# Second layer's projections with row-scaled half-precision pairs, prepared beside the scan of the third block

## The chip, the cores and the metric

The kernel runs on one NeuronCore of a Trainium2 chip. The metric is the device time of one execution in microseconds. The core has five engines with queues of their own: TensorE (PE; its weight loads are shown as PEld), VectorE (DVE), ScalarE (ACT), GpSimd (POOL) and SyncE (SP), which here only issues DMAs.

## The reference

Two layers over 2048 tokens of width 1024, one batch. The parts that the change touches are the second layer's projections; `h` is the stream after the first layer.

```python
hn = rms_norm(h, g_pre[0]);  h = x + mamba2_mixer(hn, ...)        # layer 1: projections, scan, output

# shared K/V, once
ckv, k_rope = split(rms_norm(h, g_kv_in) @ kv_w_down, [256])      # (1024 x 288)
ckv = rms_norm(ckv, g_ckv);  kv = ckv @ kv_w_up                   # k_nope, v of 16 heads

# layer 2: latent attention
hn = rms_norm(h, g_pre[1])
cq, gate = split(hn @ mla_w_in, [384])                            # (1024 x 1408)
q = rms_norm(cq, g_q) @ mla_w_uq
o = causal_attention(q, k_nope, k_rope, v) * silu(gate)
out = rms_norm(h + o @ mla_w_out, g_final)
```

`rms_norm(h, g)` scales each row of `h` by the inverse root of its mean square and each column by a gain `g`. The gain of a column of `h` is a factor on a row of the weight matrix, and the kernel puts it there.

## The kernel before

**Precision.** A product of two 32-bit matrices is made of three TensorE products: each operand is split into a high and a low part, and `mm3` (lines 83 to 87) adds high x high, high x low and low x high in PSUM. Where the operands are prepared as F32R, the splitting is done by `split` (lines 111 to 119): ScalarE copies the source to the high part, VectorE subtracts that from the source. `pair16` (lines 121 to 124) does the same into two F16 halves. F16 needs factors that bring each row into range: for the first layer `row_scale` makes from the norms of the rows of its weights a power of two per row (`rw`), puts the reciprocal on the activations' gain (`xg`), and takes the remaining common factor out of the results (`un`, `unh`).

**Stages.** The tokens go in four blocks of 512. The first layer (`mamba`, up to about 1550 us) has 16 items, a block `b` by a group `g` each. The loop body of an item runs the scan of that item (`ssd`) and beside it what comes before and after: the output projection of the item before (`outp`), the convolved and gate projections of the item after (`xbc`, `zgate`), and now and then the preparation of the next block. Each of these is a generator; the loop steps through them one after another and lets the scan go on in proportion (20 steps of the scan over the 32 steps of the others). The first block splits its weights to F32R, the second makes half-precision pairs of them (`wpair` with `b == 1`) and keeps them in DRAM (`w16_d`), the third and the fourth load those.

The second layer's projections (`mla`, about 1550 to 2080 us) run over the same four blocks: `mla_kv_down` (288 columns), `mla_cq` (384 columns), `mla_gate` in two halves of 512 channels, and `mla_up`, which makes keys, values and queries and whose steps are interleaved with the gate's, or in the first block with the last output projection of the first layer. The first half of the gate of the first block is done in the last item of `mamba`. The activations of a block come from `prep` (F32R pairs, eight tiles `xT` per block out of eight buffers). Each weight tile of kv-down, latent and gate comes from `wunit`: a DMA on SP's queue to a raw tile, a ScalarE copy that multiplies by the row's gain, a VectorE subtraction. The raw tiles have three buffers (`wraw`), the pairs six (`wsp`), shared with `mla_up` and `outp`; the gate's later halves use the scan's old tiles instead (`y`, `Xd` and `st0` to `st3`). So the same weights are loaded and split again for each of the four blocks. `latent` copies the results of the two narrow projections out of PSUM and norms them.

Attention follows from about 2080 us, then the output projection (`back`) to the end.

**Order.** The Python order of the calls is the order of priority. A planner orders each engine's queue from it, with its own estimate of durations and of when buffers come free; `high_priority(AHEAD)` puts weight loads and splits ahead of it. In attention TensorE's order is the written one.

**Buffers of the third block.** `hx` (four tiles of 128 x 1024) holds rows of the input in the third item of a block, `wraw` is used there only for a small weight of the next block's time steps.

Of the kernel before, what the change touches and what calls it, by code (L numbers as in the profile page):

```python
# [20 lines left out]
P = 128  # L21
# [26 lines left out]
)  # L48
MAGIC = 12582912.0
# [19 lines left out]
class Net:  # L69
    def __init__(self, tc, a):  # L70
        self.tc, self.nc, self.a = tc, tc.nc, a
        self.n = 0
        self.raws, self.turn = ["y", "Xd"], False
# [52 lines left out]
    def raw(self, late):  # L126
        if not late:
            return self.t(self.wp, "wraw", [P, TB], bufs=WRAW)
        self.raws = self.raws[::-1]
        return self.t(self.sp, self.raws[0], [P, TB], bufs=2)  # L130

    def wunit(self, src, n, scale=None, late=False, norm=None):


        with self.tc.high_priority(AHEAD):
            raw = self.raw(late)
            self.nc.sync.dma_start(raw[:, :n], src)
            if late:
                self.turn = not self.turn
                w = [self.t(self.sp, f"st{2 * self.turn + i}", [P, TB], F32R, bufs=1) for i in range(2)]  # L140
            else:
                u = self.unit = self.t(self.wp, "wsp", [P, 2, TB], F32R, bufs=WSP)
                w = [u[:, i, :] for i in range(2)]
# [39 lines left out]
    def row_scale(self):  # L183
# [17 lines left out]
        v.tensor_tensor(self.xg, self.g0, e.bitcast(F32), ALU.mult)  # L201
        q = self.t(self.sm, "rq", [P, KD], bufs=1)
        v.scalar_tensor_tensor(q, self.xg, -1.0, self.xg, ALU.mult, ALU.max)
# [16 lines left out]
        v.tensor_scalar(self.xg, self.xg, both[:, 0:1], None, ALU.mult)  # L220
        v.tensor_copy(self.un, both[:, 1:2])
        v.tensor_scalar(self.unh, both[:, 1:2], 0.5, None, ALU.mult)
        yield
# [51 lines left out]
    def constants(self, cp):  # L275
# [3 lines left out]

        self.mk = cp.tile([P, 2 * P], BF16, name="mk")  # L280
# [5 lines left out]
    def layer_constants(self, cp):  # L286
# [17 lines left out]
        self.xg = cp.tile([P, KD], F32, name="xg")  # L304
        self.un = cp.tile([P, 1], F32, name="un")
# [23 lines left out]
    def mamba(self, cp):  # L329
# [9 lines left out]
        for n, (b, g) in enumerate(items):  # L339
# [10 lines left out]
            if g == G - 2 and b + 1 < NB:  # L350
# [4 lines left out]
                parts += [self.prep16(b + 1), self.steps(b + 1)]  # L355
# [70 lines left out]
    def prep(self, b, gain=None, tag="tr", each=4):  # L426
# [3 lines left out]
        for k in range(KD):  # L430
            ps = self.transposed(xs, k, tag)
            u = self.t(self.xq, "xT", [P, 2, TB], F32R, bufs=8)
            self.split(u[:, 0, :], u[:, 1, :], ps, None if gain is None else gain[:, k:k + 1])
            self.xT[b].append(u)
            if k % each == each - 1:
                yield

    def prep16(self, b):

        xs = self.xn.pop(b)  # L440
        self.xT[b] = []
        for k in range(KD):
            ps = self.transposed(xs, k)
# [3 lines left out]
            self.pair16(w[:, 0, :], w[:, 1, :], ps, self.xg[:, k:k + 1])  # L447
            self.xT[b].append(w)
            if k % 4 == 3:
                yield  # L450
# [298 lines left out]
    def mla(self, early):  # L749
# [5 lines left out]
        for b in range(NB):  # L755
# [25 lines left out]
            after = iter(()) if last else self.prep(NB + b + 1, None, "mm", 1)  # L781
# [58 lines left out]
    def latent(self, banks, width, total):  # L840
# [3 lines left out]
        for i in range(4):  # L844
            nc.scalar.activation(raw[i][:, :total], banks[i][:, :total], AF.Copy)
# [16 lines left out]
    def mla_kv_down(self, b, tables):  # L862

        nc, a = self.nc, self.a
        banks = self.token_gemm(
            self.xT[NB + b],
            lambda k: self.wunit(a["kv_w_down"][k * P:(k + 1) * P, :], 288, self.gk[:, k:k + 1]), 288, "mm")
# [12 lines left out]
    def mla_cq(self, b):  # L880

        w_in = self.a["mla_w_in"]
        banks = self.token_gemm(
            self.xT[NB + b],
# [465 lines left out]
```

## Time and profile before

| | us |
|---|---|
| median of three runs (3192.35 to 3196.06) | 3196.03 |
| profiled execution | 3198.38 |
| its span, first to last instruction | 3196.6 |
| mean granted TensorE clock | 0.997 |
| TensorE busy | 3099.3 (97%) |
| TensorE weight loads busy | 2244.3 (70%) |
| VectorE busy | 2374.5 (74%) |
| ScalarE busy | 2012.7 (63%) |
| GpSimd busy | 606.6 (19%) |
| mean DMA rate | 151 GB/s |

The profile names a group of instructions by line, engine, operation and tiles (out<-in), with its count, its busy time, the mean duration in ns and the idle time of the engine before it with what ended that. Matmuls overlap in the pipeline: a 128 x 512 one is shown with 380 to 410 ns though the next starts after some 216 to 234 ns, so the distance from start to start is what a product costs. L85 to L87 are the three products of `mm3`, L115 and L116 `split` without a scale, L118 and L119 with one, L123 and L124 `pair16`, L137 the weight load of `wunit`, L845 the copy in `latent`, L648 GpSimd's subtraction in the scan.

### The profile page before, as it was taken

Reading aid. Unit: us, or ns where it says so; the run is one execution under the profiler, and the core shown is the slowest. Engines: PE = TensorE matmul, PEld = TensorE weight load, DVE = VectorE, ACT = ScalarE, POOL = GpSimd, SP = SyncE. Lnnn points to the kernel's source line nnn. Section 1 sums busy time; section 2 is a strip of 40 time slices with the busy share of each in tenths; the row PEclk is TensorE's granted clock in tenths of the full one; section 3 lists DMA queues with packets and bytes.
Section 4 is the critical chain, followed back from the end, with each engine's and each line's share of the span. In section 5 each row is a group of like instructions: output and inputs, shape, how many; then the busy total and the mean of one; then the engine's idle time right before and its main releaser. Section 6 shows DMA issues by size and latency. Waiting matters only on the chain.

```text
span 3196.6 us, 51130 instructions
## 1 busy us (share of the span) xinstructions
PE 3099.3 (97%) x17735; PEld 2244.3 (70%) x17735; DVE 2374.5 (74%) x4786; ACT 2012.7 (63%) x5027; POOL 606.6 (19%) x847
## 2 busy tenths in 40 slices
PE   8999998999999999999999999999999999999998
PEld 6777654556655566655878888877777777777777
DVE  6878887777667666767766675578888888888665
ACT  7878566665455464556646554477877778778522
POOL 1222111211121211212111211322221122222100
PEclk9999999999999999999999999999999999999999
DMA  5443657554443345534386655843434434443394
GB/s 176 127 125 121 212 205 239 191 185 152 142 158 126 115 149 178 172 126 135 125 274 232 214 196 192 267 102 79 98 78 85 80 78 97 78 99 98 109 265 156
DMA packets 220403, 482.51 MB, mean 151 GB/s; under 512 B 28976, under 2 KB 66864, under 8 KB 218704
## 3 DMA queue, kind: packets, MB, share of 16 engines
q1 hardware_dynamic: 178336, 353.78, 34.4%
q0 software_dynamic: 41808, 125.47, 16.0%
q8 instruction: 140, 2.29, 0.3%
q14 instruction: 119, 0.97, 0.1%
HBM read 347.02 MB, written 132.12 MB: 150 GB/s over the span
## 4 chain that ended last, share of the span: by engine, by line
PE 64%; DVE 9%; ACT 6%; DMA 6%; issue 2%; POOL 1%; SPq 0%; ACTq 0%; DVEq 0%; POOLq 0%
PE mm L85 13%; PE mm L86 12%; PE mm L87 12%; PE tr L1090 6%; PE tr L1100 3%; PE tr L1101 3%; PE tr L87 3%; PE tr L86 3%; PE tr L85 3%; DVE cacc L495 2%; DMA big<-cumT 1%; PE tr L699 1%; DMA wraw<-in_ssm_w_in_dram 1%; ACT Pr L1075 1%; DMA os<-ri_d 1%
## 5 line engine op out<-in xcount | busy, mean ns | idle before, releaser
L124 DVE SCALAR_TENSOR_TENSOR PTs<-tr,PTs 128x512 f16<-128x512 f32 (+3 forms) x640 | 374.6, 607 | 92.7 <-ACT PTs L123 87.1
L123 ACT ACTIVATE PTs<-tr 128x512 f16<-128x512 f32 (+3 forms) x640 | 328.2, 540 | 141.8 <-PE tr L1090 140.7
L1063 DVE TENSOR_REDUCE mx<-mm 128x1 f32<-128x512 f32 (+2 forms) x631 | 375.3, 607 | 47.2 <-PE mm L87 44.9
L1075 ACT ACTIVATE Pr<-mm,nm 128x512 f32<-128x512 f32 (+2 forms) x631 | 395.1, 635 | 23.2 <-DVE nm L1067 21.4
L1090 PE MATMUL tr<-pack,Pr 128*128 128x128 f32 x2176 | 317.8, 273 | 1.3 <-ACT Os L1107 1.2
L85 PE MATMUL mm<-xT,wsp 128*128 128x512 f16 (+1 forms) x800 | 309.8, 387 | 0.0
L85 PE MATMUL mm<-K,xT 96*128 96x512 f32 (+2 forms) x639 | 287.0, 449 | 23.2 <-ACT Pr L1075 21.6
L86 PE MATMUL mm<-xT,wsp 128*128 128x512 f16 (+1 forms) x800 | 307.0, 384 | 0.0
L87 PE MATMUL mm<-xT,wsp 128*128 128x512 f16 (+1 forms) x800 | 305.7, 384 | 0.2 <-DVE wsp L116 0.2
L1090 PEld LDWEIGHTS tr<-pack,Pr 128*128 128x128 f32 x2176 | 253.2, 141 | 50.0 <-ACT Os L1107 2.0
L85 PE MATMUL mm<-wsp,xT 128*128 128x512 f16 (+2 forms) x640 | 235.9, 370 | 3.8 <-ACT craw L489 2.8
L495 DVE SCALAR_TENSOR_TENSOR cacc<-craw,pack,cacc 128x512 f32<-128x512 f32 x288 | 218.7, 780 | 27.9 <-ACT cacc L493 25.7
L86 PE MATMUL mm<-wsp,xT 128*128 128x512 f16 (+2 forms) x640 | 235.2, 367 | 1.4 <-DVE wsp L124 1.3
L87 PE MATMUL mm<-wsp,xT 128*128 128x512 f16 (+2 forms) x640 | 234.4, 367 | 0.0
L86 PE MATMUL mm<-K,xT 96*128 96x512 f32 (+2 forms) x639 | 231.6, 363 | 0.0
L87 PE MATMUL mm<-K,xT 96*128 96x512 f32 (+2 forms) x639 | 231.4, 362 | 0.0
L1100 PE MATMUL tr<-PTs,xT 128*128 128x512 f16 (+3 forms) x640 | 222.2, 349 | 0.1
L1101 PE MATMUL tr<-PTs,xT 128*128 128x512 f16 (+3 forms) x640 | 219.7, 347 | 0.0
L85 PE MATMUL mm<-wsp,yT 128*128 128x512 f32 x512 | 209.3, 409 | 6.8 <-DMA wsp<-wo_d 4.1
L692 ACT ACTIVATE Xw<-tr,d_wend 128x64 f32<-128x64 f32 x512 | 111.7, 328 | 161.1 <-DVE y L689 134.6
L86 PE MATMUL mm<-wsp,yT 128*128 128x512 f32 x512 | 204.5, 399 | 0.0
L87 PE MATMUL mm<-wsp,yT 128*128 128x512 f32 x512 | 203.8, 399 | 0.0
(419 smaller groups left out, 7363.6 us busy)
## 6 DMA issues: line engine op xcount, KB each, us to landing
wsp<-wo_d SPq DMA_DIRECT2D x96, 512.0 KB, 3.6
wraw<-in_ssm_w_in_dram SPq DMA_DIRECT2D x128, 256.0 KB, 3.2
big<-cumT SPq DMA_DIRECT2D x64, 512.0 KB, 4.8
wsp<-w_d SPq DMA_DIRECT2D x64, 512.0 KB, 3.8
wo_d<-wsp SPq DMA_DIRECT2D x32, 512.0 KB, 3.6
w_d<-wsp SPq DMA_DIRECT2D x32, 512.0 KB, 3.6
xT<-qn_d POOLq DMA_DIRECT2D x64, 256.0 KB, 4.7
K<-kn_d POOLq DMA_DIRECT2D x15, 1024.0 KB, 8.5
```

The source lines that it names most:

```text
L85: mm(out, l_hi, r_hi, start=start, stop=False)
L86: mm(out, l_hi, r_lo, start=False, stop=False)
L87: mm(out, l_lo, r_hi, start=False, stop=stop)
L123: self.nc.scalar.activation(hi, src, AF.Copy, scale=scale)
L124: self.nc.vector.scalar_tensor_tensor(lo, src, scale, hi, ALU.mult, ALU.subtract)
L495: nc.vector.scalar_tensor_tensor(acc, raw[:, k:k + TB], wk[k], acc, ALU.mult, ALU.add)
L692: act(Xw[:, hc], px[:, hc], AF.Copy, scale=wend[:, h0 + h:h0 + h + 1])
L1063: v.tensor_reduce(mx[:, n:n + 1], s[:, :w], AX.X, ALU.max)
L1075: nc.scalar.activation(x[:, :w], s[:, :w], AF.Exp, bias=nm, accum_out=sm[:, n:n + 1])
L1090: nc.tensor.transpose(pt[:, j * P:(j + 1) * P], st["P"][j][kb], self.ident)
L1100: nc.tensor.matmul(st["O"][:, c], vals[h][:, kb, :], u[:, 0], start=kb == 0, stop=False)
L1101: nc.tensor.matmul(st["O"][:, c], vals[h][:, kb, :], u[:, 1], start=False, stop=kb == nk - 1)
```

## The change

The second layer's projections take F16 pairs. New is `keep2(ks)`: for the row tiles `ks` of the two weight matrices it loads 128 rows (gate columns to one `hx` tile, latent and kv-down columns to another), sums the squares of each row with its gains on ScalarE (three squares), makes from them a power of two per row on VectorE, splits four pieces into F16 pairs with that factor and the gain (`wraw` tiles), and stores them in the new DRAM tensor `w2_d`; each store is issued after the next piece's split. After the last tile `common`, cut out of `row_scale`, makes the activations' factors `xg2` and the common factors `un2` and `unh2`. `beside` steps `keep2` once per step of `zgate` and runs the remaining steps when `zgate` is done. It stands in the items of the third block: row tiles 0 to 2 with its first group, 3 to 5 with the second, 6 and 7 with the fourth. `w2` loads the pairs: two row tiles per DMA to a `wsp` tile, or one per DMA to one of four tiles `st0` to `st3` where the gate came late before. The activations come from `prep16` (four buffers per block), the common factor leaves with the copy in `latent`, the gate's tanh and the output scale `us`.

```diff
-    def wunit(self, src, n, scale=None, late=False, norm=None):
+    def wunit(self, src, n, scale=None, norm=None):
...
-            if late:
-                self.turn = not self.turn
-                w = [self.t(self.sp, f"st{2 * self.turn + i}", [P, TB], F32R, bufs=1) for i in range(2)]
-            else:
...
+    def keep2(self, ks):
+        nc, v, a = self.nc, self.nc.vector, self.a
+        held = []
+        for k in ks:
+            rows = slice(k * P, (k + 1) * P)
+            A, B = (self.t(self.hh, "hx", [P, D], bufs=4) for _ in range(2))
+            nc.sync.dma_start(A, a["mla_w_in"][rows, 384:1408])
+            nc.sync.dma_start(B[:, 0:384], a["mla_w_in"][rows, 0:384])
+            nc.sync.dma_start(B[:, 384:672], a["kv_w_down"][rows, :])
+            yield
+            g1, gk = self.g1[:, k:k + 1], self.gk[:, k:k + 1]
+            n = self.t(self.sm, "kn", [P, 4])
+            junk = self.t(self.wp, "wraw", [P, D], BF16, bufs=WRAW)
+            for i, (x, g) in enumerate(((A, g1), (B[:, 0:384], g1), (B[:, 384:672], gk))):
+                nc.scalar.activation(junk[:, :x.shape[1]], x, AF.Square, scale=g, accum_out=n[:, i:i + 1])
+            v.tensor_reduce(n[:, 3:4], n[:, 0:3], AX.X, ALU.add)
+            v.tensor_scalar(n[:, 3:4], n[:, 3:4], TINY * TINY, None, ALU.max)
...
+            v.tensor_tensor(f[:, 1:2], f[:, 0:1], g1, ALU.mult)
+            v.tensor_tensor(f[:, 2:3], f[:, 0:1], gk, ALU.mult)
+            yield
+            for x, g, at in ((B[:, 384:672], 2, KV2), (B[:, 0:384], 1, CQ2),
+                             (A[:, 0:512], 1, GA2), (A[:, 512:1024], 1, GA2 + 1024)):
+                c = x.shape[1]
+                u = self.t(self.wp, "wraw", [P, 2, c], F16, bufs=WRAW)
+                self.pair16(u[:, 0], u[:, 1], x, f[:, g:g + 1])
+                held.append((self.w2_d[rows, at:at + 2 * c].rearrange("p (s c) -> p s c", s=2), u))
+                if len(held) > 1:
+                    nc.sync.dma_start(*held.pop(0))
+                yield
+        nc.sync.dma_start(*held.pop(0))
+        if ks[-1] == KD - 1:
...
+            self.common(self.xg2, self.un2, self.unh2)
+            yield
+
+    def beside(main, more):
+        for _ in main:
+            next(more, None)
+            yield
+        for _ in more:
+            pass
+
+    def w2(self, at, n, k, late=False):
+        nc = self.nc
+        with self.tc.high_priority(AHEAD):
+            if late:
+                self.turn = (self.turn + 1) % 4
+                u = self.t(self.sp, f"st{self.turn}", [P, 1, 2, n], F16, bufs=1)
+                nc.sync.dma_start(u[:, 0], self.w2_d[k * P:(k + 1) * P, at:at + 2 * n].rearrange(
+                    "p (s c) -> p s c", s=2))
+                return [u[:, 0, i, :] for i in range(2)]
+            if k % 2 == 0:
+                u = self.w16 = self.t(self.wp, "wsp", [P, 2, 2, n], F16, bufs=WSP)
+                nc.sync.dma_start(u, self.w2_d[k * P:(k + 2) * P, at:at + 2 * n].rearrange(
+                    "(j p) (s c) -> p j s c", j=2, s=2))
+        return [self.w16[:, k % 2, i, :] for i in range(2)]
...
-                parts.append(self.prep(NB))
+                parts.append(self.prep16(NB, self.xg2))
...
+            elif b == NB - 2:
+                parts[-1] = self.beside(parts[-1], self.keep2({0: (0, 1, 2), 1: (3, 4, 5), 3: (6, 7)}[g]))
...
-            after = iter(()) if last else self.prep(NB + b + 1, None, "mm", 1)
+            after = iter(()) if last else self.prep16(NB + b + 1, self.xg2, "mm", 1)
...
-            nc.scalar.activation(raw[i][:, :total], banks[i][:, :total], AF.Copy)
+            nc.scalar.activation(raw[i][:, :total], banks[i][:, :total], AF.Copy, scale=self.un2)
...
-            lambda k: self.wunit(a["kv_w_down"][k * P:(k + 1) * P, :], 288, self.gk[:, k:k + 1]), 288, "mm")
+        banks = self.token_gemm(self.xT[NB + b], lambda k: self.w2(KV2, 288, k), 288, "mm")
...
+        banks = self.token_gemm(self.xT[NB + b], lambda k: self.w2(CQ2, 384, k), 384, "tr")
...
-            return self.wunit(self.a["mla_w_in"][k * P:(k + 1) * P, c0:c0 + 512], 512, self.g1[:, k:k + 1], b + n > 0)
+            return self.w2(GA2 + n * 1024, 512, k, b + n > 0)
...
-            nc.scalar.activation(sz, bank, AF.Tanh, scale=0.5)
+            nc.scalar.activation(sz, bank, AF.Tanh, scale=self.unh2)
...
+            v.tensor_scalar(us, us, self.un2, None, ALU.mult)
```

More of the change, by code (lines that the diff above doesn't have):

```diff
@@ L48 @@
 )
+KV2, CQ2, GA2, ALL2 = 0, 576, 1344, 3392
 MAGIC = 12582912.0
@@ L72, in __init__ @@
         self.n = 0
-        self.raws, self.turn = ["y", "Xd"], False
+        self.turn = 0
     def name(self, s):
@@ L354, in mamba @@
                     parts = parts[1:] + parts[:1] + [self.row_scale()]
-                parts += [self.prep16(b + 1), self.steps(b + 1)]
+                parts += [self.prep16(b + 1, self.xg), self.steps(b + 1)]
                 total += 3
@@ L424, in load_x, with prep, prep16 @@
                     nc.vector.tensor_scalar(v, v, r[:, i:i + 1], None, ALU.mult)
-    def prep(self, b, gain=None, tag="tr", each=4):
+    def prep(self, b, gain):
+        xs = self.xn.pop(b)
+        self.xT[b] = []
+        for k in range(KD):
+            ps = self.transposed(xs, k)
+            u = self.t(self.xq, "xT", [P, 2, TB], F32R, bufs=8)
+            self.split(u[:, 0, :], u[:, 1, :], ps, gain[:, k:k + 1])
+            self.xT[b].append(u)
+            if k % 4 == 3:
+                yield
+    def prep16(self, b, factors, tag="tr", each=4):
         xs = self.xn.pop(b)
@@ L431, in prep @@
             ps = self.transposed(xs, k, tag)
[L432 to L443, printed above, removed]
             if k % 2 == 0:
```

52 lines of the change are left out of this document (29 added, 23 removed).

## The prediction

> **What bounds the kernel now.** I read the page's first two parts, then a table of the stretches that the change touches, then the groups of instructions and the order of time inside them.
>
> ```profile
> PE 3099.3 (97%) x17735; PEld 2244.3 (70%) x17735; DVE 2374.5 (74%) x4786; ACT 2012.7 (63%) x5027; POOL 606.6 (19%) x847
> PE   8999998999999999999999999999999999999998
> PEclk9999999999999999999999999999999999999999
> ```
>
> TensorE is busy nearly everywhere at the full granted clock. So the time falls only if TensorE's stream gets shorter or its few gaps close, and it rises only if new gaps open. Columns of the next table: length, then busy us (and count) of PE, PEld, DVE, ACT, POOL, then clock, DMA share, GB/s.
>
> ```profile
> 40.00:360.00 320.00, 314.97 (x1744) 249.94 (x1743) 255.03 (x461) 252.63 (x670) 64.03 (x79) 1.00 0.43 132
> 400.00:790.00 390.00, 368.82 (x2154) 219.50 (x2152) 306.73 (x530) 248.29 (x588) 72.88 (x93) 0.99 0.59 194
> 490.00:590.00 100.00, 90.52 (x502) 52.83 (x501) 73.70 (x125) 60.19 (x138) 18.95 (x24) 0.98 0.64 212
> 815.00:905.00 90.00, 90.00 (x534) 54.23 (x533) 57.91 (x97) 45.98 (x117) 18.43 (x24) 1.00 0.51 176
> 905.00:995.00 90.00, 89.60 (x531) 53.99 (x530) 57.79 (x97) 46.24 (x118) 18.83 (x24) 1.00 0.38 129
> 1105.00:1190.00 85.00, 82.79 (x513) 52.12 (x512) 59.42 (x116) 48.23 (x124) 13.31 (x15) 1.00 0.42 141
> 1550.00:1640.00 90.00, 83.84 (x451) 71.90 (x450) 55.32 (x135) 42.63 (x91) 13.22 (x21) 0.98 0.60 195
> 1640.00:2082.00 442.00, 439.33 (x2175) 371.04 (x2174) 291.56 (x558) 233.21 (x432) 87.04 (x142) 1.00 0.69 226
> ```
>
> Rows 1 and 2 are the first and second blocks of tokens, row 3 the worst stretch of the second. Rows 4 to 6 are the scans of the third block beside which the new work is put: TensorE idles 0, 0.4 and 2.2 us there, 2.6 us of 265. Rows 7 and 8 are the second layer's projections: 6.2 us idle while they start, then 2.7 us of 442. They are a pure TensorE stretch, so a faster matmul there should arrive in the total.
>
> **Part 1: the matmuls' type.** The kv-down, query-latent and gate projections turn from pairs of 32-bit to pairs of half-precision operands; their number stays: three products of 8 row tiles by 4 banks by 4 blocks, 384 each of 288 and of 384 columns, and twice that, 768, of 512 columns. First a stretch of 32-bit products (columns: start, duration), then one of half-precision ones in the first layer.
>
> ```profile
> 1905.05 0.39 PE L85 MATMUL tr<-xT,st 128*128 128x512 f32 x1
> ...
> 1909.71 0.40 PE L87 MATMUL mm<-yT,wsp 128*128 128x512 f32 x1
> ```
>
> ```profile
> 821.82 0.38 PE L85 MATMUL mm<-wsp,xT 128*128 128x512 f16 x1
> ...
> 823.98 0.38 PE L86 MATMUL mm<-wsp,xT 128*128 128x512 f16 x1
> ```
>
> The first pair has 20 starts between its rows: 4.66 / 20 = 233 ns from start to start. The second has 10: 2.16 / 10 = 216 ns. So 17 ns go from each of 768 products: 13.1 us. The groups kept apart by shape (busy us, mean ns) give the rest:
>
> ```profile
> L85 PE MATMUL tr<-xT,st 128*128 128x512 f32 x128 | 52.2, 408 | 0.0
> L86 PE MATMUL tr<-xT,st 128*128 128x512 f32 x128 | 50.4, 394 | 0.0
> L85 PE MATMUL mm<-xT,wsp 128*128 128x512 f16 x576 | 218.9, 380 | 0.0
> L85 PE MATMUL tr<-wsp,xT 128*128 128x384 f32 x128 | 43.1, 337 | 0.0
> L1100 PE MATMUL tr<-PTs,xT 128*128 128x384 f16 x64 | 20.9, 326 | 0.0
> L87 PE MATMUL mm<-wsp,xT 128*128 128x288 f32 x128 | 37.2, 295 | 0.0
> L1100 PE MATMUL tr<-PTs,xT 128*128 128x256 f16 x64 | 17.6, 275 | 0.0
> ```
>
> The ends are modelled, so I use only differences of like groups. 384 columns: 337 against 326, 11 ns by 384 = 4.2 us. 288 columns have no half-precision row: between 275 (256 columns) and 326 (384) lies 275 + 32 x 51 / 128 = 288, against 295; 7 ns by 384 = 2.7 us. The first product of a triple after transposes of 32-bit tiles is longer (408 against 394, so 14 x 128 = 1.8 us) and the half-precision rows show no such thing. Part 1 is 13.1 + 4.2 + 2.7 + 1.8 = **21.8 us gained**; 13.1 if only the wide ones gave, 28.0 if the 768 narrow ones gave 17 ns each too.
>
> The Trainium skill, TensorE: Matmul & The Clock Gate (Wait — 56ns, not 53.3ns?), puts a warm stream at columns / 2.4 + 2.5 ns, 215.7 ns for 512, whatever the operands. By it part 1 would be nothing and the sum below +1.7 us, 3198; the 233 ns above decide against that, so it gets no chance of its own, and the half-precision 216 agree.
>
> **Part 2: the splitting of weights leaves the projections.** One ScalarE copy and one VectorE subtraction for each of 128 weight tiles go (64 for the gate, 32 and 32 for the narrow ones):
>
> ```profile
> L118 ACT ACTIVATE wsp<-wraw,pack 128x384 fp32r<-128x384 f32 x32 | 18.7, 615 | 20.2 <-DMA wraw<-in_mla_w_in_dram 14.2 <-PE mm L87 4.2 <-PE tr L87 1.3
> L118 ACT ACTIVATE wsp<-wraw,pack 128x288 fp32r<-128x288 f32 x32 | 17.0, 536 | 26.6 <-DMA wraw<-in_kv_w_down_dram 18.8 <-PE mm L87 7.2
> ```
>
> With 0.72 for a gate tile (the 512-column copy in part 3), ScalarE loses 64 x 0.72 + 32 x 0.615 + 32 x 0.536 = 83 us, VectorE about as much. They were covered by TensorE, so in themselves worth nothing. They do cost at the start, where three raw buffers serve kv-down, query latent and up-projection in turn. ScalarE, then TensorE:
>
> ```profile
> 1589.15 0.63 ACT L115 ACTIVATE wsp<-wraw 128x512 fp32r<-128x512 f32 x1 [2.40 <-DMA wraw<-in_kv_w_up_dram]
> ```
>
> ```profile
> 1590.22 0.66 PE L271 MATMUL tr<-pack,xs 128*128 128x128 f32 x4 [2.00 <-ACT xs L845]
> ...
> 1592.12 0.63 PE L86 MATMUL mm<-wsp,yT 128*128 128x512 f32 x1
> 1592.55 0.63 PE L87 MATMUL mm<-wsp,yT 128*128 128x512 f32 x1
> ```
>
> ScalarE stands 2.40 us for an up-projection weight; the latent's copies (L845) queue behind, and TensorE loses 2.00 us and then starts products 0.43 us apart instead of 0.23, at the half clock that shows as 0.98 in row 7: 2.0 + 0.02 x 90 = **3.8 us**. With kv-down and query latent off the raw buffers that weight can be fetched long before, so I book all of it. Bounds: 0, and the whole idle of that row with the clock loss, 6.2 + 1.8 = 8.0. What is late next there is the first layer's last output weights, a wait that I leave:
>
> ```profile
> PE mm L85 <- DMA wsp<-wo_d: 4.1, 3, 1.9
> ```
>
> The DMAs: as many bytes (two half-precision halves are as long as one 32-bit word), 92 loads instead of 128 (kv-down and query latent by pairs of tiles). Nothing on TensorE. Likewise the activations' half-precision pairs take four buffers per block instead of eight, and the scale from a column costs ScalarE some 0.1 us a copy, hidden as above.
>
> **Part 3: the new work beside the third block.** `keep2` does three row tiles in each of the first two scans, two in the fourth. Per row tile: two 32-bit loads' worth in three DMAs, three squares with sums (1024, 384, 288 columns), nine column-sized VectorE operations, four pairs (288, 384, 512, 512), four stores. Nearest rows:
>
> ```profile
> L263 ACT ACTIVATE yt<-hx 128x1024 bf16<-128x1024 f32 x28 | 29.2, 1045 | 3.9 <-DMA hx<-in_x_dram 3.8
> L263 ACT ACTIVATE yt<-xs 128x384 bf16<-128x384 f32 x16 | 8.2, 528 | 0.1
> L263 ACT ACTIVATION_READ_ACCUMULATOR yt<-xs 128x1 f32 x32 | 6.5, 205 | 0.0
> L123 ACT ACTIVATE wsp<-wraw,rw 128x512 f16<-128x512 f32 x64 | 45.1, 720 | 26.2 <-DMA wraw<-in_ssm_w_in_dram 24.5 <-PE tr L93 1.5
> L124 DVE SCALAR_TENSOR_TENSOR wsp<-wraw,rw,wsp 128x512 f16<-128x512 f32 x64 | 48.9, 773 | 16.2 <-ACT wsp L123 16.0
> L119 DVE SCALAR_TENSOR_TENSOR wsp<-wraw,pack,wsp 128x384 fp32r<-128x384 f32 x32 | 19.2, 615 | 13.6 <-ACT wsp L118 13.5
> L119 DVE SCALAR_TENSOR_TENSOR wsp<-wraw,pack,wsp 128x288 fp32r<-128x288 f32 x32 | 16.4, 515 | 24.9 <-ACT wsp L118 24.9
> L254 DVE SCALAR_TENSOR_TENSOR rsy<-rsq,rsy 128x4 f32<-128x4 f32 x105 | 16.7, 159 | 2.3
> ```
>
> ScalarE: 1.05 + 0.53 + 0.45 (an estimate for 288 from the 384 row) + 3 x 0.2 + 2 x 0.72 + 0.615 + 0.536 = 5.2 us, by eight 42 us. VectorE: 2 x 0.773 + 0.615 + 0.515 + 9 x 0.16 = 4.1 us, by eight 33 us. Over the three scans ScalarE goes from 140.4 to 182 us of 265 (0.69), VectorE from 175.1 to 208 (0.78). No product waits for any of it, so by itself it is hidden in what those engines have left. But a scan's own chain runs over both, and `beside` hands out one step of `keep2` per step of the gate projection (8), while three tiles have 18 steps: some ten steps come in one heap before the scan's tail and the next scan. What such a load costs is read from two stretches. Row 1 has VectorE at 255 / 320 = 0.80 and ScalarE at 0.79, and TensorE idles 5.0 / 320 = 1.6%. Row 2 has 0.79 and 0.64 and idles 21.2 / 390 = 5.4%, but there its own weights are being split and products wait for them. On 265 us: 4.2 to 14.4 us, less today's 2.6, so +1.6 to +11.8. I take **+5**, a third of the way, since no product waits for `keep2`.
>
> Loads and stores: three tiles are 2.6 MB in and 2.6 MB out per 90 us, 58 GB/s on top of 176 and 129. The projections live with 226 GB/s at 0.6% idle, so no term. The two TensorE instructions of `common` come once; I book +0.5 for them, between 0 and 2.
>
> **Sum**: -21.8 - 3.8 + 5 + 0.5 = -20.1. The profiled execution took 3198.4 us (span 3196.6); 3198.4 - 20.1 = 3178.3. The runs' median, 3196.0, lies 2.4 below that execution, so 3175.9; I say **3176**. With all bounds: -28.0 - 8 + 1.6 = -34.4 to -13.1 + 11.8 + 2 = +0.7, 3162 to 3197; the likeliest case's own range, with not all of them at one end, is 3166 to 3189.
>
> **Rivals.** (A) *The scan's chain gives it back.* Each chunk's state goes through GpSimd's subtractions:
>
> ```profile
> L648 POOL TENSOR_TENSOR Sp<-st,Sp 128x512 fp32r<-128x512 f32 x15 | 22.0, 1468 | 52.4 <-ACT Sp L647 52.3
> ```
>
> ```profile
> L648 POOL TENSOR_TENSOR Sp<-st,Sp 128x512 fp32r<-128x512 f32 x8 | 10.2, 1276 | 24.0 <-ACT Sp L647 24.0
> ```
>
> The first row is the second block (400 to 790), the second the third (815 to 995): beside half-precision splitting the same operation is 0.19 us longer. With ScalarE's and VectorE's queues late as well, the scans could fall to the worst stretch, 9.5 idle of 100: 265 x 0.095 - 2.6 = 22.6 us, so -21.8 - 3.8 + 22.6 + 0.5 = -2.5, 3193.5, no change. Against it: row 1, as loaded, idles 1.6%. The Trainium skill, SBUF — State Buffer (Who interferes with whom), holds that VectorE with two SBUF inputs and GpSimd lock each other out of a shared port pair for a whole instruction. By it, 32 subtractions of up to 0.77 us could hold GpSimd 25 us in all, about the same time; the 0.19 us that rows show is a quarter of one such instruction.
>
> (B) *The projections become bound by something else*, the evictions or stores of the up-projection, and half of part 1 turns into waits: -10.9 - 3.8 + 5.5 = -9.2, 3187. For it: DMA share 0.69. Against: VectorE falls from 292 of 442 us, ScalarE too.
>
> (C) *Slower: SP's queue.* `keep2` issues its 24 loads and 32 stores there, among the loads of the third block's own kept weights, and a store that waits for VectorE holds back the loads behind it. If a store cost TensorE 1.2 us, 32 would cost 38 us: -21.8 - 3.8 + 0.5 + 38 = +12.9, 3209. It decides from 25.1 / 32 = 0.8 us a store. Against it, SP already stands on VectorE for long in the projections, where TensorE idles 2.7 us:
>
> ```profile
> SPq L137 <- DVE st L119: 139.5, 41, 9.9
> ```
>
> (D) The change does not do what it says, the half-precision products running no faster here: excluded as far as the first layer's half-precision stretch above shows 216 ns.
>
> **How the numbers follow.** The forecast has 0.76, (A) 0.08, (B) 0.08, (C) 0.06, more than all bounds of gain 0.02. A measurement here tells 0.2%, 6.4 us, from no change: faster means below 3189.6. That holds for the forecast nearly whole, (B) and the last: 0.84; the same, (A) and the forecast's rim: 0.10; slower, (C): 0.06. The range reaches from 3164 to 3192, past (B) and short of (A) and (C).
>
> **What would show it.** Gate products at 216 ns, 17 to 25 us less between the start of kv-down and the first scores; no row of weight splitting there; TensorE's 2.0 us before L845's transposes gone. The three scans of the third block longer by 2 to 12 us, together, with VectorE near 0.78. I am wrong if the third block grows by over 20 us, if SP's waits there have weight loads queued behind stores, or if the projections keep their length with new idle before evictions.

## The result, and the profile after

The changed kernel took 3173.98 us (median of 4 runs, 3168.60 to 3176.22) against 3196.05 (4 runs, 3192.35 to 3199.24) beside it: ratio 0.9929, 95% interval 0.9912 to 0.9946. 3176.0 was forecast. The profiled execution took 3176.22 us, its span is 3174.4, 22.2 less than before.

I cut both spans at five marks that both kernels have: the issue of the scan's load of E (`big<-cumT`) for the first item of the third and of the fourth block, the first product of 288 columns, the first product of the scores, the last transpose of attention. Windows of the kernel before between these marks (start and end, length, then busy us and count of PE, PEld, DVE, ACT, POOL, then clock, DMA share, GB/s):

```profile
0.00:809.60 809.60, 766.55 (x4363) 523.66 (x4363) 634.03 (x1163) 565.00 (x1422) 149.97 (x194) 1.00 0.54 172
809.60:1183.40 373.80, 369.99 (x2187) 222.84 (x2188) 250.27 (x441) 198.96 (x496) 73.37 (x96) 1.00 0.41 139
809.60:899.50 89.90, 89.90 (x533) 54.23 (x534) 57.81 (x98) 46.47 (x118) 18.42 (x24) 1.00 0.51 176
899.50:990.10 90.60, 90.20 (x533) 54.24 (x534) 57.94 (x98) 46.57 (x119) 19.34 (x25) 1.00 0.38 128
...
1183.40:1557.70 374.30, 369.48 (x2212) 232.01 (x2212) 261.26 (x442) 204.62 (x516) 82.95 (x102) 1.00 0.44 147
1557.70:2081.90 524.20, 515.37 (x2564) 436.71 (x2562) 340.72 (x681) 270.08 (x510) 97.75 (x160) 1.00 0.68 222
2081.90:3004.80 922.90, 898.27 (x5648) 686.49 (x5647) 771.39 (x1829) 732.65 (x2008) 201.74 (x296) 1.00 0.41 85
```

and of the kernel after:

```profile
0.00:810.50 810.50, 765.27 (x4363) 523.98 (x4363) 642.78 (x1202) 577.73 (x1452) 151.53 (x193) 1.00 0.54 177
810.50:1189.80 379.30, 371.71 (x2188) 223.85 (x2187) 268.27 (x509) 220.46 (x547) 72.48 (x97) 1.00 0.49 164
810.50:905.60 95.10, 91.90 (x534) 55.27 (x534) 69.40 (x137) 59.00 (x149) 19.26 (x24) 0.98 0.68 232
905.60:995.80 90.20, 89.90 (x533) 54.16 (x533) 57.87 (x98) 46.50 (x118) 17.59 (x25) 1.00 0.38 129
...
1189.80:1563.20 373.40, 368.14 (x2214) 223.86 (x2215) 255.81 (x446) 198.79 (x503) 80.13 (x102) 1.00 0.45 151
1563.20:2061.90 498.70, 494.41 (x2562) 333.04 (x2561) 275.31 (x560) 208.70 (x394) 103.78 (x168) 1.00 0.70 232
2061.90:2983.40 921.50, 897.68 (x5648) 687.62 (x5647) 771.74 (x1829) 731.89 (x2008) 197.66 (x289) 1.00 0.41 84
```

The stretch of the projections is 25.5 us shorter. The third block is 5.5 longer, and its first item carries 5.2 of that: 89.9 to 95.1, VectorE 57.8 to 69.4 us. The second item has the same VectorE work as before, 98 instructions: no tile of `keep2` lies there. All other stretches agree within 1.5 us. These lengths come from one execution each, so a difference of 1.5 us between two kernels says little.

**The projections.** Products of the changed kernel, of 512 columns, then of 384, then of 288:

```profile
1881.68 0.39 PE L86 MATMUL mm<-xT,st 128*128 128x512 f16 x1
...
1882.98 0.38 PE L86 MATMUL mm<-xT,st 128*128 128x512 f16 x1
```

```profile
1578.75 0.33 PE L88 MATMUL tr<-wsp,xT 128*128 128x384 f16 x1
...
1581.35 0.33 PE L86 MATMUL tr<-wsp,xT 128*128 128x384 f16 x1
```

```profile
1565.82 0.29 PE L88 MATMUL mm<-wsp,xT 128*128 128x288 f16 x1
...
1568.40 0.29 PE L88 MATMUL mm<-wsp,xT 128*128 128x288 f16 x1
```

From start to start: 6 in 1.30 us, 216 ns; 16 in 2.60, 162; 21 in 2.58, 123. The kernel before, at 384 and at 288 columns:

```profile
1573.76 0.34 PE L86 MATMUL tr<-wsp,xT 128*128 128x384 f32 x1
...
1576.88 0.34 PE L86 MATMUL tr<-wsp,xT 128*128 128x384 f32 x1
```

```profile
1559.88 0.30 PE L85 MATMUL mm<-wsp,xT 128*128 128x288 f32 x1
...
1560.95 0.30 PE L87 MATMUL mm<-wsp,xT 128*128 128x288 f32 x1
```

18 in 3.12, 173 ns; 8 in 1.07, 134 ns. So the type gives 17, 11 and 11 ns a product. What TensorE waited for most in this stretch (total us, times, longest), before and after:

```profile
PE tr L271 <- ACT xs L845: 4.5, 5, 2.0
PE mm L85 <- DMA wsp<-wo_d: 4.1, 3, 1.9
```

```profile
PE mm L86 <- DMA wsp<-wo_d: 3.8, 2, 2.4
```

All five waits before the latent's transposes are gone; the one for the first layer's output weights stays.

**The third block.** The subtractions of `keep2` in the changed kernel (count, shortest, median and longest ns, first and last start), and the one large gap of TensorE in the first item:

```profile
L125 DVE SCALAR_TENSOR_TENSOR wraw<-hx,kw,wraw x32: 508/680/752, 758.6 to 1166.9; 128x512 f16<-128x512 f32 x16, 128x288 f16<-128x288 f32 x8, 128x384 f16<-128x384 f32 x8
```

```profile
833.67 0.38 PE L88 MATMUL mm<-wsp,xT 128*128 128x512 f16 x1
836.98 1.60 PE L772 MATMUL tr<-Xd,big 128*64 128x64 f32 x32 [2.93 <-DVE big L751]
...
839.97 0.65 PE L86 MATMUL mm<-wsp,xT 128*128 128x512 f16 x1
840.41 0.62 PE L87 MATMUL mm<-wsp,xT 128*128 128x512 f16 x1
840.84 0.41 PE L88 MATMUL mm<-wsp,xT 128*128 128x512 f16 x1
```

The first subtraction starts at 758.6, 52 us ahead of the third block: the planner takes the tiles as soon as the `hx` buffers are free. In the trace three tiles lie in the last item of the second block, three in the first item of the third, none in the second, two in the last. The gap is a wait for VectorE's multiplication of E, and behind it products start 0.43 us apart until 841, at half the rate.

### The profile page after: what moved, and what is told of

Read it like the earlier page. It is cut to its first block, busy times and chain, and to the rows that moved or that the text cites. A ratio compares the mean times of both kernels' runs of the same rounds, so it can differ in the third digit from the quotient of the medians.

```text
span 3174.4 us, 50942 instructions
## 1 busy us (share of the span) xinstructions
PE 3077.0 (97%) x17738; PEld 2135.0 (67%) x17738; DVE 2330.3 (73%) x4777; ACT 1978.9 (62%) x4979; POOL 606.4 (19%) x847
## 4 chain that ended last, share of the span: by engine, by line
PE 64%; DVE 9%; ACT 7%; DMA 5%; issue 2%; POOL 1%; SPq 0%; ACTq 0%; DVEq 0%; POOLq 0%
PE mm L86 12%; PE mm L88 12%; PE mm L87 12%; PE tr L1158 6%; PE tr L1168 3%; PE tr L1169 3%; PE tr L88 3%; PE tr L87 3%; PE tr L86 3%; DVE cacc L568 2%; DMA big<-cumT 2%; DMA wraw<-in_ssm_w_in_dram 1%; PE tr L772 1%; ACT Pr L1143 1%; ACT big L749 1%
## 5 line engine op out<-in xcount | busy, mean ns | idle before, releaser
L1143 ACT ACTIVATE Pr<-mm,nm 128x512 f32<-128x512 f32 (+2 forms) x631 | 394.9, 635 | 23.1 <-DVE nm L1135 21.5
L1131 DVE TENSOR_REDUCE mx<-mm 128x1 f32<-128x512 f32 (+2 forms) x631 | 375.6, 607 | 45.8 <-PE mm L88 42.9
L86 PE MATMUL mm<-K,xT 96*128 96x512 f32 (+2 forms) x639 | 287.0, 449 | 23.1 <-ACT Pr L1143 21.8
```

The source lines that it names most:

```text
L86: mm(out, l_hi, r_hi, start=start, stop=False)
L1131: v.tensor_reduce(mx[:, n:n + 1], s[:, :w], AX.X, ALU.max)
L1143: nc.scalar.activation(x[:, :w], s[:, :w], AF.Exp, bias=nm, accum_out=sm[:, n:n + 1])
```

## The experiments

Lengths are of each run's profiled execution, cut as above; "first" and "second" are items of the third block.

| kernel | median, us | ratio to before (95%) | start to third block | first | second | third block | to kv-down | to scores |
|---|---|---|---|---|---|---|---|---|
| before | | | 809.6 | 89.9 | 90.6 | 373.7 | 374.3 | 524.2 |
| after | 3173.98 | 0.9929 (0.9912 to 0.9946) | 810.5 | 95.1 | 90.2 | 379.3 | 373.4 | 498.7 |
| e_keep32 | 3215.08 | 1.0050 (1.0037 to 1.0063) | 810.2 | 93.2 | 91.1 | 379.8 | 375.4 | 529.6 |
| e_split16 | 3183.80 | 0.9955 (0.9942 to 0.9968) | 808.6 | 90.2 | 90.1 | 373.1 | 379.8 | 504.0 |
| e_keep_alone | 3205.81 | 1.0027 (1.0015 to 1.0038) | 809.1 | 94.9 | 90.1 | 379.4 | 377.9 | 524.8 |
| e_spread | 3176.77 | 0.9933 (0.9920 to 0.9947) | 811.2 | 94.5 | 90.3 | 379.9 | 374.3 | 498.6 |
| e_paced | 3182.40 | 0.9947 (0.9934 to 0.9960) | 810.0 | 95.3 | 95.1 | 386.9 | 375.0 | 499.6 |
| e_eprio | 3174.24 | 0.9918 (0.9905 to 0.9932) | 808.1 | 95.5 | 90.1 | 379.3 | 375.6 | 498.7 |
| e_nosub | 3202.10 | 1.0010 (1.0000 to 1.0019) | 810.9 | 92.7 | 90.3 | 376.3 | 378.1 | 523.0 |
| e_nostore | 3204.21 | 1.0017 (1.0007 to 1.0028) | 809.9 | 94.0 | 90.3 | 378.0 | 377.1 | 523.0 |
| e_place | 3174.53 | 0.9923 (0.9909 to 0.9936) | 808.9 | 92.9 | 90.5 | 378.0 | 377.3 | 499.9 |
| e_pool | 3194.83 | 0.9988 (0.9979 to 0.9997) | 815.1 | 100.7 | 90.0 | 389.8 | 375.6 | 497.3 |
| e_both | 3200.47 | 1.0009 (1.0000 to 1.0017) | 817.4 | 95.7 | 90.4 | 389.2 | 381.7 | 499.2 |
| e_lasts | 3195.83 | 0.9991 (0.9982 to 0.9999) | 826.3 | 91.1 | 90.3 | 376.7 | 379.5 | 499.4 |

### Type or relief: e_keep32, e_split16

My theory was that the type makes most of the gain and the splitting that leaves only removes a stall; the rival, that taking the splitting away is what helps. `e_keep32` keeps 32-bit pairs, so nothing is split in the projections but the type stays. `e_split16` has the half-precision type, and splits the weights again in each block; beside the third block it only sums squares and makes factors. Edits against the kernel after, shortened:

```diff
 e_keep32
-                u = self.t(self.wp, "wraw", [P, 2, c], F16, bufs=WRAW)
-                self.pair16(u[:, 0], u[:, 1], x, f[:, g:g + 1])
+                    u = self.t(self.wp, "wraw", [P, 2, c], F32R, bufs=WRAW)
+                    self.split(u[:, 0], u[:, 1], src[:, cs], g)
...
 e_split16
-                nc.sync.dma_start(u[:, 0], self.w2_d[k * P:(k + 1) * P, at:at + 2 * n].rearrange(
-                    "p (s c) -> p s c", s=2))
...
+            nc.sync.dma_start(raw[:, :n], src)
+            self.pair16(u[:, 0], u[:, 1], raw[:, :n], self.f2[:, k, g:g + 1])
```

> Weights of the second layer's three projections are split once beside the third block and kept in DRAM, but as 32-bit pairs; the products stay 32-bit, squares and factors are left out. My theory (the gain is the product's spacing, 17, 11 and 8 to 12 ns): the stretch from the first kv-down product to the first scores, 524.2 us before and 498.7 after, stays at 518 to 522 (only the 2.0 us stall and its half clock go), the third block grows by 2 to 6 us from 373.7, total 3194 to 3199. Rival (the gain is ScalarE's and VectorE's relief from splitting): that stretch falls to 498 to 503, total about 3176. If twice the bytes of weights hurt, the stretch is over 524.

> Half-precision products, but the weights are loaded raw and split again in each of the four blocks; beside the third block stand only the loads, squares and row factors (no pairs, no stores). My theory: the stretch from kv-down to the scores falls by the products alone, from 524.2 to 500 to 504 us, the stall before the up-projection (2.0 us at L845's transposes) is back, third block +1 to +3, total 3174 to 3180. Rival (relief from splitting): the stretch stays at 520 to 524, total 3196 to 3199.

The type alone takes the stretch from 524.2 to 504.0, and the rival falls: without splitting but with 32-bit products it is 529.6, 5.4 longer than before, a loss that I had only as a side branch (its time, 3215.08, is above both theories). TensorE's longest wait there, of `e_keep32` (`w_d` is the DRAM tensor of the kept pairs) and of `e_split16`:

```profile
PE mm L86 <- DMA wsp<-w_d: 8.1, 4, 5.0
```

```profile
PE tr L328 <- ACT xs L910: 4.0, 2, 2.4
```

With twice the bytes to load (DMA share 0.81 in this stretch, 0.68 before) the kept pairs themselves come late. Less these 8.1 us the stretch would be 521.5, still far from the rival's 498 to 503. And with the splitting back in place, the wait before the latent's transposes is back (4.0 us; L910 is the copy in `latent` there). So the 5.3 us between 504.0 and 498.7 belong to the kept pairs, and that wait is 4.0 of them. The time of `e_split16`, 3183.80, is above the 3174 to 3180 that I gave: its fourth block is 5.5 us longer than before, which the part on the prediction takes up.

### What the third block pays: e_keep_alone, e_nosub, e_nostore

`e_keep_alone` is the kernel before with `keep2` beside its third block and the results unused; the other two leave the low halves or the stores out of it (edits against `e_keep_alone`, shortened).

```diff
 e_nosub
-                self.pair16(u[:, 0], u[:, 1], x, f[:, g:g + 1])
-                held.append((self.w2_d[rows, at:at + 2 * c].rearrange("p (s c) -> p s c", s=2), u))
+                nc.scalar.activation(u[:, 0], x, AF.Copy, scale=f[:, g:g + 1])
+                held.append((self.w2_d[rows, at:at + c], u[:, 0]))
 e_nostore
-                if len(held) > 1:
-                    nc.sync.dma_start(*held.pop(0))
...
-        nc.sync.dma_start(*held.pop(0))
```

> The kernel before with the new work beside the third block added and its results unused: the second layer loads, splits and multiplies as before. My theory: the third block grows from 373.7 to 378 to 380 us, all else as before, total 3200 to 3203 (+5). Rival (hidden in idle time of ScalarE and VectorE): total 3196. Rival (SP's queue): +10 or more, with weight loads behind stores.

> The kernel before with keep2 beside its third block and the results unused, as the run of keep2 alone had it, but without the subtractions on VectorE: only the high halves are made and stored, half the bytes; the 32 low halves are left out. If VectorE's subtractions cost the third block its time: 373-375 us there against 379.4 with them, the time 3197-3201 us. If the loads, the stores or ScalarE's 42 us do: 377-380 us there, the time 3202-3206 us.

> The kernel before with keep2 beside its third block and the results unused, but without the stores to DRAM; loads, squares, factors and pairs stay. If VectorE's subtractions cost the third block its time: 378-380 us there, as with the stores, and the time 3202-3206 us. If the stores cost it (their issues on SyncE's queue or their 7 MB): 373-376 us there, the time 3197-3201 us.

`e_keep_alone` shows the block's loss without the rest of the change: 379.4, 5.7 over before; its total, 3205.81, is above the 3200 to 3203 that I gave, with the fourth block's stretch 3.6 longer as well. What the loads, squares and factors cost beside the first item is not shown: in `e_split16` (373.1) none of them lies there, the squares of six tiles run before the third block and those of two in its last two items. Without the subtractions the block takes 376.3, without the stores 378.0: 3.1 and 1.4 of the 5.7 us, the second no more than unchanged stretches differ. `e_nostore` came out as the theory of the subtractions said. `e_nosub` landed between its two branches for the block; it also stores half as much, so the 3.1 us are not the subtractions' alone. So the subtractions are the largest part that was found, not the whole. Of the 2.6 us that remain without them, ScalarE's squares and copies and the other stores may have a part; none was tried alone.

### Collision or load: e_spread, e_paced, e_eprio

The gap at 836.98 suggested one collision: `keep2`'s subtractions and the convolution ahead of E on VectorE. Three edits were to move it. `e_spread` hands the steps over evenly in the written order, `e_paced` also holds each tile's loads back until the scan chunk beside it has issued its own, `e_eprio` puts the multiplications of E ahead.

```diff
 e_paced
+            with self.tc.issue_after(self.eload.ins):
                 nc.sync.dma_start(A, a["mla_w_in"][rows, 384:1408])
...
+                    while kept * total < left * step and kept < left:
+                        next(more, None)
+                        kept += 1
 e_eprio
+            with self.tc.high_priority(60):
                 v.tensor_tensor(CB, pb[:, P:2 * P], self.triu, ALU.mult)
...
+            with self.tc.high_priority(60):
                 v.tensor_tensor(E, E, CB.unsqueeze(1).to_broadcast([P, 8, P]), ALU.mult)
```

> The changed kernel, with the steps of keep2 handed out over all 32 steps of an item in place of one per step of the gate projection and the rest in a heap. Theory 1 (the heap costs: TensorE's 2.9 us wait at the scan's first products of the third block and the half clock behind it): that wait goes, the third block falls from 379.3 to 374 to 376 us, total about 3170. Theory 2 (the load costs wherever it stands): the third block stays at 378 to 381, total 3174.

> The kernel after, with keep2 handed over every step of its item and each tile's three loads held back until the scan chunk beside it has issued its own load, so that the eight tiles really lie in their items instead of six of them in the last item of the second block and the first of the third. Collision theory (the 5.6 us of the third block are one meeting of keep2's VectorE subtractions with a convolution in the first item, where the scan's multiplication of E comes 3 us late and TensorE's clock halves behind the gap): the third block falls from 379 to 374-377 us and the time to 3169-3172 us, the gap at the first item's products below 1 us. Rival (each tile takes its 0.7 us of the busy engines wherever it lies): the third block stays at 379-380 us, the loss now spread over three items at about 2 us each, the time 3173-3177 us.

> The kernel after, with the scan's two multiplications on VectorE that make E for the products (CB by the triangle, E by CB) put ahead of other ready VectorE work in the written order; keep2 is unchanged. Theory that the multiplication of E queued behind the convolution and keep2's subtractions is what costs the third block its 5.6 us: the gap of 2.9 us ahead of the first item's products goes below 1 us, the third block takes 374-376 us and the time is 3168-3171 us, or less if scans of other blocks gain too. Rival (VectorE and ScalarE are simply fuller, and another wait takes this one's place): the third block stays at 378-380 us and the time at 3173-3177 us.

`e_spread` changes nothing: the planner pulls the tiles to the same places. `e_eprio` closes the large gap to 1.2 us and the first item still takes 95.5, as another wait of 1.6 us opens behind it and the granted clock is 0.98 again. `e_paced` does put the tiles where they were written, but for two of the 32 subtractions, which still run ahead of the third block, and misses both branches: 386.9. The windows of its first two items:

```profile
810.00:905.30 95.30, 90.23 (x523) 53.67 (x522) 66.66 (x126) 55.88 (x141) 18.24 (x25) 0.98 0.65 219
905.30:1000.40 95.10, 90.63 (x533) 54.19 (x534) 70.71 (x137) 59.52 (x148) 18.76 (x25) 1.00 0.58 193
```

Three tiles in the second item cost it 4.5 to 5 us, just as three in the first. How it comes about can be seen in `e_paced` at another place, VectorE, then TensorE's waits in the third block:

```profile
878.90 1.87 DVE L125 SCALAR_TENSOR_TENSOR wraw<-hx,kw,wraw 128x288 f16<-128x288 f32 x3
880.69 0.28 DVE L117 TENSOR_TENSOR Bt<-tr,Bt 128x128 fp32r<-128x128 f32 x1
880.89 0.28 DVE L754 TENSOR_TENSOR CB<-tr,pack 128x128 f32<-128x128 f32 x1
881.21 1.23 DVE L758 TENSOR_TENSOR big<-big,CB 128x1024 f32<-128x1024 f32 x1
```

```profile
PE tr L95 <- POOL Xp L728: 4.0, 4, 1.7
PE tr L779 <- DVE big L758: 3.6, 2, 2.0
PE tr L779 <- DVE Xd L766: 2.2, 2, 1.9
```

Three subtractions back to back stand before the scan's chain of small steps, and TensorE waits at the end of that chain; another time it is the next link. So the single collision falls as the cause; it is one form of a queue that is late.

### Other places, another engine: e_place, e_pool, e_both, e_lasts

The tiles in the second block's last item seemed to cost nothing: in all runs so far the third block begins at 808.1 to 811.2 us, 809.6 before. So `e_place` hands over four tiles beside the last items of the second and of the third block, `e_lasts` two, three and three beside those of the first three. `e_pool` gives the subtractions to GpSimd, which first scales the rows in place; `e_both` is `e_place` and `e_pool` together.

```diff
 e_place
-            elif b == NB - 2:
-                parts[-1] = self.beside(parts[-1], self.keep2({0: (0, 1, 2), 1: (3, 4, 5), 3: (6, 7)}[g]))
+            elif b in (1, 2) and g == G - 1:
+                parts[-1] = self.beside(parts[-1], self.keep2(range(4 * b - 4, 4 * b)))
 e_lasts
+            elif g == G - 1 and b < NB - 1:
+                parts[-1] = self.beside(parts[-1], self.keep2(((0, 1), (2, 3, 4), (5, 6, 7))[b]))
 e_pool
-                self.pair16(u[:, 0], u[:, 1], x, f[:, g:g + 1])
+                nc.gpsimd.tensor_scalar(x, x, f[:, g:g + 1], None, ALU.mult)
+                nc.scalar.activation(u[:, 0], x, AF.Copy)
+                nc.gpsimd.tensor_tensor(u[:, 1], x, u[:, 0], ALU.subtract)
```

> The kernel after with keep2's tiles handed over beside the last items of the second and the third block, four each, in place of three, three and two beside three items of the third. Theory that it matters beside which item a tile lies (three tiles cost some 5 us in a block's first or second item and at most 1 us in a block's last): the first item of the third block goes back from 95 to 90-91 us, the third block takes 374-376 us, the stretch up to it gains at most 1 us (810-812), the time is 3169-3172 us. Rival (a tile costs the same wherever it lies, 0.7 us): the loss moves into the second block's end and the third's last item, in sum as in the kernel after, 3173-3176 us.

> The kernel after with keep2's work taken off VectorE: GpSimd scales the raw rows in place and subtracts, ScalarE makes the high half as before. If VectorE's fullness makes half of the third block's loss: its first item goes from 95 to 92-93 us, the third block to 375-377 us, the time to 3170-3173 us. Rival (the scan loses as much to GpSimd, whose own steps of the scan are then queued behind keep2's 64 instructions): the third block stays at 379 us or above, the time at 3174-3180 us.

> Both edits together: keep2 beside the last items of the second and third block, and its subtractions on GpSimd. If both theories hold: the third block at 373-375 us and the time at 3167-3171 us. If GpSimd's queue costs what VectorE's did: as the placed version alone or some us above it, 3170-3178 us.

> The kernel after with keep2's tiles beside the last items of the first three blocks: two, three and three. In the runs so far three tiles beside the second block's last item left the start of the third block where it was (808.9 to 811.2 us against 809.6) and two or three beside the third block's last item cost 1 us, while one to three tiles in a first item cost 3 to 5 us. If that holds for every last item and no tile slides on into a first one: the third block takes 374-376 us, its start stays at 809-812 us, the stretch to the projections 373-375 us, the time is 3168-3171 us. Rival (the loss is the same 5 us in sum wherever the tiles lie, and takes another place each time, as with four and four): 3173-3177 us.

In `e_place` one tile of the first four slides into the third block's first item (92.9) and one of the other four into the fourth block's first, which takes 100.3 us instead of 96.6: the time is that of the kernel after, as the rival said. Where VectorE makes half-precision pairs, the first item takes 91.1 us with no tile in it (`e_lasts`; 89.9 before), 92.9 with one, 94.0 to 95.5 with three.

GpSimd is no refuge. Its groups of `e_pool` from 750 to 1190 us:

```profile
L254 POOL TENSOR_SCALAR hx<-hx,kw 128x512 f32<-128x512 f32 x16 | 25.1, 1579 | 0.0
L256 POOL TENSOR_TENSOR wraw<-hx,wraw 128x512 f16<-128x512 f32 x16 | 20.9, 1310 | 4.2 <-ACT wraw L255 4.2
```

A wide piece costs 2.9 us there against VectorE's 0.75, and the convolution's halo copies and the scan's subtractions are queued behind: third block 389.8, and the time 3194.83 is far above both branches. `e_both` is dearer still, 3200.47, and misses its branches too.

In `e_lasts` the third block comes close to the theory: its first item is back at 91.1, the block at 376.7, for 374 to 376. But the first two tiles slide into the second block's first item, the third block begins 16.7 us late, and the time misses both branches. The second block's first two items, before and in `e_lasts`:

```profile
409.60:511.70 102.10, 98.10 (x562) 57.04 (x563) 82.64 (x136) 69.08 (x164) 19.25 (x25) 1.00 0.72 241
511.70:614.30 102.60, 92.68 (x532) 54.33 (x530) 77.09 (x128) 62.96 (x148) 20.68 (x26) 0.98 0.59 193
```

```profile
406.40:514.40 108.00, 92.51 (x501) 54.11 (x502) 76.24 (x146) 72.49 (x178) 18.56 (x22) 0.94 0.69 231
514.40:626.90 112.50, 104.05 (x591) 59.85 (x592) 88.97 (x144) 69.88 (x159) 21.67 (x28) 1.00 0.65 208
```

Two tiles cost 16 us where the second block splits its own weights. Both lie in the first item, and only there TensorE's idle time rises, from 4.0 to 15.5 us (9.9 and 8.5 in the second, which takes over some 60 products), with a granted clock of 0.94. Its longest waits there are for VectorE's steps of the scan, 8.9 us, then 4.3 for the block's own half-precision pairs. So VectorE's late queue shows there too; what part the three shared raw buffers have was not tried. No version was measurably faster than the changed kernel; `e_eprio` (0.9918) and `e_place` (0.9923) lie within its interval.

## Why the prediction was right, and where its steps were not

**Part 1** gave 21.8 us; the measured spacings give 768 x 17 + 384 x 11 + 384 x 11 = 21.5. Two terms were off and cancelled, which was luck. The 288 columns were put at 7 ns between modelled durations and measured 11: 4.2 for 2.7. The first product of a triple after transposes was put at 1.8 us, from 408 against 394 ns, and is worth nothing; the last section shows why. `e_split16` shows the part by itself: -20.2. As for the rule from the Trainium skill that was weighed there (TensorE: Matmul & The Clock Gate, Wait — 56ns, not 53.3ns?), the half-precision products agree with its 215.7 ns and the 32-bit ones, at 233, do not. The section names no type of operand; that its figure holds for all of them was my reading.

**Part 2** gave 3.8 us, and what is left of the 25.5 is 4.0. The mechanism stands, shown both ways by the wait at the latent's transposes. Its size was put together otherwise: one wait of 2.0 and the clock behind it, where the four smaller waits of the same kind, 2.5 us together, went too. The wait for the output weights stayed, as said. That splitting is worth nothing where TensorE covers it stands as well.

**Part 3** gave +5 and `common` +0.5; the third block took +5.5. The step that failed is the even spreading, "beside" three scans that get longer together with VectorE near 0.78. The planner moved the tiles: the first item alone is longer, VectorE at 69.4 / 95.1 = 0.73 there, and three tiles fell into the second block. The price was read from the idle share at a load, over 265 us; what the runs show is a price per tile that depends on its neighbours: some 1.7 us in a first or second item of the third block (5.2 / 3, and `e_paced`), little in a last one (third and fourth item together 0.7 us longer for two tiles, in `e_paced` 3.2), 8 in the second block's first item. With the tiles in the items where I had put them (`e_paced`), the third block is 13.2 longer, above my bound of 11.8; but that is the slowest of the run's six executions, 4.6 above their median, so whether the bound was passed is open. `e_paced` is the dearer place in any case: ratio 0.9947 (0.9934 to 0.9960) against 0.9918 (0.9905 to 0.9932) of `e_eprio`, measured beside it. So the sum was right with luck in the place. `common` cost a wait of 0.69 us in the fourth block, where I had put 0.5; in `e_split16`, with VectorE late, it was 2.99, over my bound of 2. With the half clock behind that gap (0.97 granted over the item of 102 us, some 3 us) it is all that this kernel lost there (379.8).

**Rivals.** (A) did not come, but its mechanism shows. GpSimd's subtraction has the same mean in the same window (815 to 995 us) as before, 1275 ns for 1276, but that tests nothing: none of those eight overlaps a subtraction of `keep2`. The one that does, in the last item, takes 1.65 us; its like before took 1.29:

```profile
1160.56 0.61 DVE L125 SCALAR_TENSOR_TENSOR wraw<-hx,kw,wraw 128x384 f16<-128x384 f32 x1
...
1160.66 1.65 POOL L721 TENSOR_TENSOR Sp<-st,Sp 128x512 fp32r<-128x512 f32 x1 [2.62 <-ACT Sp L720]
```

```profile
1154.08 1.29 POOL L648 TENSOR_TENSOR Sp<-st,Sp 128x512 fp32r<-128x512 f32 x1 [2.08 <-ACT Sp L647]
```

Behind the large gap of the first item it is the scan's own steps that meet, and VectorE is held up as well, 1.65 us for an operation that takes 0.75 elsewhere:

```profile
842.13 1.72 POOL L721 TENSOR_TENSOR Xp<-Xw,Xp 128x512 fp32r<-128x512 f32 x1
...
842.76 1.65 DVE L795 SCALAR_TENSOR_TENSOR y<-y,un,sz 128x512 f32<-128x512 f32 x1
```

These rows agree with the shared port pair (the Trainium skill, SBUF — State Buffer, Who interferes with whom). What was wrong with the 25 us is how often the two meet: of the scan's wide GpSimd subtractions in the third block 5 of 33 took over 1.4 us, 1 of 31 before, 1.3 us more in sum. (B) is false: 232 GB/s and DMA share 0.70 with nothing new waited for. At 0.81, in `e_keep32`, something else does bind, but it is the loads of the kept pairs, not the evictions or stores that (B) named. (C): the stores cost some 1.4 us in all, 0.04 a store against the 0.8 from which it would have decided, though SP stood on `keep2`'s subtractions for long:

```profile
SPq L257 <- DVE wraw L125: 22.9, 13, 3.3
```

(D) is excluded by the 216 ns.

## What to carry to other kernels

Price a type change by start-to-start spacing in each shape, not by modelled durations. Work that nothing waits for still costs what it delays in front of it in an engine's queue, so price it by the item in which the trace shows it run, which is not where it is written, and expect moving it to move the wait rather than remove it. Weights that are split once and kept paid here with half-precision pairs, as long as the raw ones; with 32-bit pairs, twice as long, they lost.

## What the hardware showed unexpectedly

Where the type changes, single starts mislead. A change from half-precision products to 32-bit ones in the kernel after:

```profile
1883.85 0.38 PE L87 MATMUL mm<-xT,st 128*128 128x512 f16 x1
1884.06 0.38 PE L88 MATMUL mm<-xT,st 128*128 128x512 f16 x1
1884.09 0.58 PE L86 MATMUL tr<-wsp,BC 128*128 128x512 f32 x1
1884.51 0.39 PE L87 MATMUL tr<-wsp,BC 128*128 128x512 f32 x1
```

The first 32-bit product starts 0.03 us behind the last half-precision one and takes 0.42: together 0.45, just 0.216 + 0.233. The longer first product is paid by a shorter one ahead of it, so the change itself costs nothing. Behind the transposes of 32-bit tiles, where I had booked 1.8 us, it is the same: in the kernel before, a product at 1651.84 us starts 0.03 us behind the last transpose and the next one follows after 0.31, together 0.34, just the 0.11 of a transpose and 0.233. So my 1.8 us was no cost that could go. And in the kernel after, behind a TensorE gap of 2.93 us the products started 0.43 us apart, twice their 0.216, until 841, some 4 us behind the gap: by an estimate from these spacings that adds about 2 us to it.
